# Gate strips of a Conformer-convolution layer loaded back through GpSimd's queue into four buffers

## The chip, the cores and the metric

One core of a Trainium2 chip runs the whole program. The metric is device time in microseconds (us) of one execution; for the kernel before, the median of 3 runs is 1468.54 us (1467.7 to 1470.9).

## The reference, cut to what matters

Two residual layers over 1040 tokens (16 meta tokens and 1024 others) of width 1024: a Conformer convolution, then differential attention, then a final RMSNorm. The change lies in the first layer:

```python
proj = h @ w_in                                   # 1024 -> 3 * 2048
u, g, z = split(proj, 3)
v = depthwise_causal_conv31(u * sigmoid(g)) + dw_bias
v = silu(layer_norm(v, ln_gain, ln_bias))         # over the 2048 channels
h = h + (v * silu(z)) @ w_out                     # 2048 -> 1024
```

`silu(z)` is the gate. It is needed only once the norm over all channels is known, so the kernel parks it in DRAM and loads it back.

## The kernel before, in words

Channels stand on partitions. The 2048 convolution channels are 16 strips (i or k, 0 to 15) of 128; the 1040 tokens are split by parity, and each parity half again into two halves n = 0 and 1 (HT = 520, QT = 260 elements). Every fp32 operand of a matmul is split in a high part (ScalarE copy, `wh`, `hi`) and a remainder (`lo_part`, L157, `wl`, `lo`), and `passes` (L207) multiplies high*high, high*low and low*high.

The first layer goes through these steps.

- Convolution, strips 0 to 15 (L457 to L534): TensorE makes the two projections, `vr{i}` holds the gated strip (tag `vr`, VR = 2 buffers), ScalarE and GpSimd make products and sums for part of the taps into `pb{i}` (tag `pa`, 2 buffers, L496 and L511), VectorE does the other taps (L524) and joins all (L526 to L528).
- Gates: `z_gate` (L431) projects z, applies SiLU and writes the strip to DRAM (`sz_d`, L441, from ScalarE's queue). Strips 0 to 11 are done beside the convolution, 12 to 15 after it (L587). The last, 15, is run strip by strip of the input (`release`), so that the buffers of the layer's input come free one by one.
- Norm: `mean` (L584), `center(0)` (subtract L558, square L563, sum `sq_sum` L564), `token_scale(0)` (`var_ps` L547, L573 to L578).
- First half, `y_part(k, 0)` (L596): for each even k one load `szr` brings two strips of the gate back (L601); each strip is scaled (L612), goes through SiLU (L613) and is multiplied by the gate (L621, all 16 on VectorE as `YM` says). `operand(0, k)` splits it into the two parts `b` (L638 on ScalarE, L639 by `lo_part` on VectorE).
- Output projection, half 0: strips m = 0 and 1 side by side, then m = 2 to 7, each 16 k of 6 matmuls (`multiply`, L655), residual added in `add_residual` (L664; `xr` is loaded on SP's queue, L666). Its weights take two strips each; the one numbered 50 (m = 0, k = 8 to 15) puts its remainder `wl50` into a buffer of tag `vr` (L182, `STW`).
- Beside half 0's projection, the norm of the other half, `center(1)` and `token_scale(1)` (L718), and then `y_part(k, 1)` and `operand(1, k)`, three or four k behind each m (`OK`, L736). Here 14 of the 16 products L621 are on GpSimd, those of k = 3 and k = 7 on VectorE. Tiles `y`, `xr` and `hsq` share three buffers (tag `xs`).
- Output projection, half 1, then the attention layer.

All DMAs that the table below names come from three queues: SP (weights `wf` L173, `szr`, `xr`), ScalarE's (`sz_d`) and GpSimd's (only in the attention layer and at the end, L968, L969, L1198). A queue runs its instructions in order, DMA issues too. A planner fixes that order when the program is built (`schedule_with_timeline_sim=True`): it runs a model of the engines and takes, on each, the ready instruction of the highest priority, which is program order moved forward by `high_priority` and held back by `issue_after`. Buffers of a tag are handed out in that order.

Of the kernel before, what the change touches and what calls it, by code (L numbers as in the profile page):

```python
# [12 lines left out]
F32 = mybir.dt.float32  # L13
# [6 lines left out]
P = 128  # L20
# [22 lines left out]
VR = 2  # L43
# [52 lines left out]
def trunk(  # L96
# [16 lines left out]
    V, A, G, PE, SP = nc.vector, nc.scalar, nc.gpsimd, nc.tensor, nc.sync  # L113
# [25 lines left out]
    def small(name, w, bufs=4):  # L139
        return scratch[-1].tile([P, w], F32, tag="sm", name=name, bufs=bufs)  # L140
# [164 lines left out]
    with ExitStack() as st0:  # L305
        sb = st0.enter_context(tc.tile_pool(name="sb0", bufs=1))
# [6 lines left out]
        def buf(tag, name, dt=F32, bufs=2):  # L313
            return sb.tile([P, T], dt, tag=tag, name=name, bufs=bufs)
# [106 lines left out]
        QT = HT // 2  # L421

        def part(t, n):

            return t.rearrange("p (two s) -> p two s", two=2)[:, :, n * QT : n * QT + QT]
# [31 lines left out]
        for i in range(CT):  # L457
            vr = sb.tile([P, 2, PAD + HT], F32, tag="vr", name=f"vr{i}", bufs=VR)
# [6 lines left out]
            with tc.high_priority(offset=HP):  # L465
                for ci, ((c0, w, o), (_, _, u)) in enumerate(zip(gates, ups)):
                    s = small(f"sig{i}", w=w)
# [128 lines left out]
        def y_part(k, n, last):  # L596
            i = k
            if k % 2 == 0:
                szr.append(sb.tile([P, 2, 2, QT], F32, tag="pa", name=f"szr{k}_{n}", bufs=2))
                with tc.issue_after(*loads[-1:]) if loads else ExitStack():  # L600
                    load = SP.dma_start(  # L601
                        out=szr[-1].rearrange("p i two s -> p i (two s)"),
                        in_=sz_d[n, i : i + 2].rearrange("i p c -> p i c"),
                    )
                loads.append(load.ins)
            s = szr[-1][:, k % 2]
            t = part(v_t[i], n)
            src = t
            if n:
                t = sb.tile([P, 2, QT], F32, tag="xs", name=f"y{k}_{n}", bufs=3)  # L610
            with tc.issue_after(done[-LOOK]) if n else ExitStack():
                y_mult.append(V.tensor_tensor(out=t, in0=src, in1=part(ln_r, n), op=ALU.mult).ins)  # L612
            silu = A.activation(  # L613
                out=t, in_=t, func=AF.Silu, scale=chn[:, i, TAPS + 1 : TAPS + 2],
                bias=chn[:, i, TAPS + 2 : TAPS + 3],
            ).ins
            y_silu.append(silu)
            if last:
                with tc.issue_after(silu):
                    A.preload_act_table_set("natural_log_exp_and_others")  # L620
            (V if n * CT + k in YM else G).tensor_tensor(out=t, in0=t, in1=s, op=ALU.mult)  # L621
            return t

        szr, loads, y_silu, y_mult = [], [], [], []

        def operand(n, ks):

            for k in ks:
                full = y_part(k, 1, k == CT - 1) if n else full0[k]
                if n:  # L630
                    t = sb.tile([P, 2, HT], F32R, tag="big", name=f"b{n}_{k}", bufs=16)
                else:
                    if k % 2 == 0:
                        twos.append(hn(f"b{n}_{k}", (P, 2, 2, HT), last=k == CT - 2))
                    t = twos[-1][:, k % 2]
                b[n].append((t[:, 0], t[:, 1]))
                hi, lo = nat(t[:, 0]), nat(t[:, 1])
                A.activation(out=hi, in_=full, func=AF.Copy)  # L638
                done.append(lo_part(V, lo, full, hi.bitcast(F32)).ins)  # L639
# [63 lines left out]
        for k in range(CT + LEAD):  # L703
            if k < CT:
                full0.append(y_part(k, 0, False))
            if k >= LEAD:
                operand(0, [k - LEAD])
# [35 lines left out]
    with ExitStack() as st1:  # L743
        sb = st1.enter_context(tc.tile_pool(name="sb1", bufs=1))
# [554 lines left out]
```

## Time and profile before

| | |
|---|---|
| median of 3 runs | 1468.54 us |
| profiled execution | 1467.64 us |
| its span | 1465.5 us |
| TensorE busy, share of the span | 97% |
| VectorE, ScalarE, GpSimd busy | 76%, 61%, 55% |
| mean granted TensorE clock | 0.991 |
| the 16 `szr` loads, 520 KB each, SP's queue | issued from 504.2 to 678.0 us |

The profile is of one execution; its span is the time from the first to the last instruction, and 2.1 us lie around it. An idle time of an engine is named with what ended it. A busy TensorE is not TensorE at its peak, since its matmuls are pipelined.

### The profile page before, as it was taken

What the parts mean: (1) busy time and instruction counts of PE and PEld (TensorE: products, weight loads), DVE (VectorE), ACT (ScalarE), POOL (GpSimd) and SP (SyncE); (2) the same over time, 40 slices, a digit from 0 to 9 for tenths busy, and PEclk for the clock granted to TensorE, in tenths of its full rate; (3) what the DMA queues carried; (4) which work ended last, traced back from release to release, by engine and by line L of the source; (5) the groups of instructions that cost most, each with busy time, mean ns of one, the idle gap of its engine ahead of it and who ended that gap; (6) DMA issues with size and microseconds to landing.
All of it is one profiled execution on the core that took longest, in us unless ns stands there. A gap on an engine that the chain in (4) does not pass through costs nothing.

```text
span 1465.5 us, 24123 instructions
## 1 busy us (share of the span) xinstructions
PE 1423.4 (97%) x8828; PEld 1333.3 (91%) x8828; DVE 1115.3 (76%) x2100; ACT 887.3 (61%) x1615; POOL 811.7 (55%) x646
## 2 busy tenths in 40 slices
PE   8999999999999999999999999999999999999997
PEld 7999999999999999899999878988889899897786
DVE  7989899899899988979545311578788787786774
ACT  7565665565555658766324411568778777786652
POOL 4598999999999940035014500525345354353572
PEclk9999999999999999999999999999999999999998
DMA  5021112112211333554443634223221322338532
GB/s 182 30 73 44 58 52 66 44 44 67 64 44 44 102 108 95 190 166 147 165 167 124 204 99 125 59 73 106 84 81 62 114 80 77 109 88 296 166 121 95
DMA packets 79928, 150.82 MB, mean 103 GB/s; under 512 B 6977, under 2 KB 46402, under 8 KB 78786
## 3 DMA queue, kind: packets, MB, share of 16 engines
q1 hardware_dynamic: 66706, 126.69, 27.3%
q0 software_dynamic: 3824, 13.37, 2.8%
q10 hardware_dynamic: 9280, 9.23, 2.0%
q8 instruction: 69, 1.13, 0.3%
q14 instruction: 49, 0.40, 0.1%
HBM read 106.73 MB, written 34.01 MB: 96 GB/s over the span
## 4 chain that ended last, share of the span: by engine, by line
PE 47%; POOL 18%; DVE 14%; ACT 8%; issue 8%; DMA 4%; SPq 1%; POOLq 0%; DVEq 0%; ACTq 0%
POOL pb L511 16%; PE c L207 8%; PE v L207 6%; PE k L207 5%; PE q L207 4%; PE za L207 4%; PE ao L207 3%; PE o L207 3%; PE u L207 3%; PE z L207 2%; DVE wl L157 2%; PE s L989 2%; ACT pr L510 2%; PE s L990 2%; PE tp L1023 2%
## 5 line engine op out<-in xcount | busy, mean ns | idle before, releaser
L511 POOL TENSOR_TENSOR pb<-pr,pb 128x521 f32<-128x521 f32 (+1 forms) x272 | 389.2, 1440 | 24.9 <-ACT pr L510 10.4
L510 ACT ACTIVATE pr<-vr,chn 128x521 f32<-128x521 f32 x224 | 150.6, 725 | 122.5 <-POOL pb L511 122.1
L207 PE MATMUL c<-b,wh 128*128 128x260 f32 x1024 | 187.3, 285 | 3.0 <-DVE b L157 1.9
L524 DVE SCALAR_TENSOR_TENSOR ev<-vr,chn,ev 128x520 f32<-128x520 f32 x240 | 181.2, 755 | 1.2
L189 ACT ACTIVATE wh<-wf 128x1024 fp32r<-128x1024 f32 x115 | 121.0, 1053 | 99.6 <-PE c L207 54.0
L207 PEld LDWEIGHTS c<-b,wh 128*128 128x128 f32 x1024 | 159.7, 191 | 3.8 <-DVE b L157 2.1
L207 PE MATMUL g<-hp,wh 128*128 128x346 f32 (+1 forms) x752 | 151.8, 329 | 7.6 <-ACT hp L383 3.6
L207 PE MATMUL u<-hp,wh 128*128 128x346 f32 (+1 forms) x752 | 155.9, 321 | 2.0 <-ACT wh L189 2.0
L207 PE MATMUL c<-b,wl 128*128 128x260 f32 x512 | 145.4, 286 | 3.8 <-DVE wl L157 3.8
L157 DVE TENSOR_TENSOR wl<-wf,wh 128x1024 fp32r<-128x1024 f32 x81 | 118.4, 1463 | 30.3 <-ACT wh L189 29.5
L157 POOL TENSOR_TENSOR wl<-wf,wh 128x1024 fp32r<-128x1024 f32 x34 | 85.7, 2521 | 92.9 <-ACT wh L189 47.4
L207 PEld LDWEIGHTS g<-hp,wh 128*128 128x128 f32 x752 | 127.6, 193 | 9.5 <-ACT hp L383 3.9
L207 PE MATMUL z<-hp,wh 128*128 128x346 f32 (+1 forms) x768 | 135.6, 321 | 0.5 <-ACT sig L469 0.5
L524 DVE SCALAR_TENSOR_TENSOR od<-xs,wc,od 128x520 f32<-128x520 f32 x176 | 132.6, 754 | 0.0
L696 POOL TENSOR_TENSOR total<-hsq,total 128x520 f32<-128x520 f32 x12 | 20.6, 1714 | 196.2 <-ACT hsq L695 196.2
L207 PEld LDWEIGHTS u<-hp,wh 128*128 128x128 f32 x752 | 125.7, 188 | 2.8 <-ACT wh L189 2.8
L207 PEld LDWEIGHTS z<-hp,wh 128*128 128x128 f32 x768 | 124.3, 188 | 0.9 <-ACT sig L469 0.7
L997 ACT ACTIVATE p<-p,st 128x272 f32<-128x272 f32 (+7 forms) x128 | 100.5, 785 | 39.3 <-DVE st L992 38.8
L207 PEld LDWEIGHTS c<-b,wl 128*128 128x128 f32 x512 | 97.7, 191 | 4.6 <-DVE wl L157 4.4
L207 PE MATMUL g<-hp,wl 128*128 128x346 f32 (+1 forms) x376 | 84.2, 322 | 0.0
L207 PE MATMUL v<-wv,g 128*128 128x512 f32 x352 | 83.5, 394 | 0.0
L989 PE MATMUL s<-k,q 128*128 128x256 f32 (+6 forms) x224 | 77.2, 349 | 5.3 <-DVE st L992 5.3
(292 smaller groups left out, 3465.1 us busy)
## 6 DMA issues: line engine op xcount, KB each, us to landing
wf<-conv_in SPq DMA_DIRECT2D x48, 512.0 KB, 3.5
wf<-conv_out SPq DMA_DIRECT2D x32, 512.0 KB, 4.1
wf<-attn_in SPq DMA_DIRECT2D x32, 512.0 KB, 3.8
wf<-attn_out SPq DMA_DIRECT2D x17, 512.0 KB, 3.7
sz_d<-sz ACTq DMA_DIRECT2D x32, 260.0 KB, 4.4
szr<-sz_d SPq DMA_DIRECT2D x16, 520.0 KB, 4.4
v<-v_d POOLq DMA_DIRECT2D x8, 1024.0 KB, 5.3
ya_d<-yb SPq DMA_DIRECT2D x28, 256.0 KB, 2.5
```

The costliest lines, as they stand in the source:

```text
L157: return eng.tensor_tensor(out=out_, in0=full, in1=hi, op=ALU.subtract)
L189: A.activation(out=wh, in_=wf, func=AF.Copy)
L207: PE.matmul(o, a[k], b[k], start=start and i == 0, stop=stop and i == tot - 1)
L510: A.activation(out=d, in_=src, func=AF.Copy, scale=w)
L511: G.tensor_tensor(out=dst, in0=d, in1=dst, op=ALU.add)
L524: V.scalar_tensor_tensor(out=dst, in0=src, scalar=w, in1=dst, op0=ALU.mult, op1=ALU.add)
L696: (V if SQA[m] == "V" else G).tensor_tensor(out=total[:, ns], in0=sq, in1=total[:, ns], op=ALU.add)
L989: PE.matmul(o[:, :wm], q2[m][:, qs], k2[m][:, c0 : c0 + wm], start=True, stop=False)
L990: PE.matmul(o[:, :wm], q2[m][:, qs], kl2[m][:, c0 : c0 + wm], start=False, stop=True)
L997: A.activation(out=p[:, :n], in_=p[:, :n], func=AF.Exp, scale=-1.0, bias=least, accum_out=st[:, 1:2],)
L1023: PE.transpose(tp[:, (kb - kb0) * P : (kb - kb0 + 1) * P], p0[:, kb * P : (kb + 1) * P], ident)
```

## The change

In the first half (n = 0) the loads of k = 2, 6, 10 and 14 go into buffers of tag `vr`, those of k = 0, 4, 8 and 12 stay in tag `pa`, so that four buffers of two strips serve the eight loads. In the second half all eight stay in `pa`. All sixteen loads are issued on GpSimd's queue in place of SP's.

```diff
         def y_part(k, n, last):
             i = k
             if k % 2 == 0:
-                szr.append(sb.tile([P, 2, 2, QT], F32, tag="pa", name=f"szr{k}_{n}", bufs=2))
+
+                if n == 0 and k % 4:
+                    szr.append(buf("vr", f"szr{k}_{n}", bufs=VR).rearrange("p (i two s) -> p i two s", i=2, two=2))
+                else:
+                    szr.append(sb.tile([P, 2, 2, QT], F32, tag="pa", name=f"szr{k}_{n}", bufs=2))
                 with tc.issue_after(*loads[-1:]) if loads else ExitStack():
-                    load = SP.dma_start(
+                    load = G.dma_start(
                         out=szr[-1].rearrange("p i two s -> p i (two s)"),
                         in_=sz_d[n, i : i + 2].rearrange("i p c -> p i c"),
                     )
```

## Rows read from the trace of the kernel before

**Rows 1.** The page, busy time of TensorE over the whole span

```profile
PE 1423.4 (97%) x8828; PEld 1333.3 (91%) x8828; DVE 1115.3 (76%) x2100; ACT 887.3 (61%) x1615; POOL 811.7 (55%) x646
```

**Rows 2.** Stretches: length, busy us (count) of PE, PEld, DVE, ACT, POOL, clock, DMA

```profile
590.50:594.60 4.10, 1.07 (x5) 0.42 (x3) 4.10 (x8) 4.05 (x7) 0.00 (x0) 0.87 0.60 182
594.60:600.20 5.60, 5.58 (x26) 5.59 (x27) 5.60 (x8) 4.24 (x7) 0.00 (x0) 0.50 0.87 290
600.20:624.00 23.80, 23.80 (x200) 23.80 (x200) 22.82 (x35) 14.02 (x21) 0.00 (x0) 1.00 0.58 184
...
692.00:694.00 2.00, 0.97 (x8) 0.97 (x9) 2.00 (x2) 1.98 (x2) 1.17 (x1) 1.00 0.05 10
```

**Rows 3.** Timeline of TensorE: start, length, instruction, [idle before it, what ended it]

```profile
592.28 0.39 PE L207 MATMUL c<-b,wh 128*128 128x260 f32 x1 [0.90 <-ACT wh L189]
594.62 0.59 PE L207 MATMUL c<-b,wh 128*128 128x260 f32 x1 [1.94 <-DVE b L157]
...
693.03 0.39 PE L207 MATMUL c<-b,wl 128*128 128x260 f32 x1 [2.23 <-DVE wl L157]
```

**Rows 4.** Timeline of VectorE, 579.9 to 623.8 us

```profile
579.91 2.52 DVE L621 TENSOR_TENSOR v<-v,szr 128x520 f32<-128x520 f32 x4
582.36 4.96 DVE L558 TENSOR_TENSOR v<-v,mean 128x520 f32<-128x520 f32 x8
...
588.38 3.74 DVE L558 TENSOR_TENSOR v<-v,mean 128x520 f32<-128x520 f32 x6
592.04 1.91 DVE L621 TENSOR_TENSOR v<-v,szr 128x520 f32<-128x520 f32 x3
593.87 0.69 DVE L157 TENSOR_TENSOR b<-v,b 128x520 fp32r<-128x520 f32 x1
...
597.54 2.35 DVE L157 TENSOR_TENSOR wl<-wf,wh 128x1024 fp32r<-128x1024 f32 x2
...
604.08 1.29 DVE L621 TENSOR_TENSOR v<-v,szr 128x520 f32<-128x520 f32 x2
...
616.73 7.05 DVE L564 TENSOR_TENSOR sq_sum<-sq_sum,lsq 128x520 f32<-128x520 f32 x9
```

**Rows 5.** Timeline of ScalarE, the high parts of the first operands

```profile
585.72 1.24 ACT L638 ACTIVATE b<-v 128x520 fp32r<-128x520 f32 x2
```

**Rows 6.** Timeline of SP's queue, DMA issues

```profile
581.25 1.59 SPq L601 DMA_DIRECT2D szr<-sz_d  x2
...
651.44 0.38 SPq L601 DMA_DIRECT2D szr<-sz_d  x1
```

**Rows 7.** Timeline of GpSimd around the first half and in the second

```profile
508.50 20.43 POOL L511 TENSOR_TENSOR pb<-pr,pb 128x521 f32<-128x521 f32 x14
...
629.55 1.31 POOL L696 TENSOR_TENSOR total<-hsq,total 128x520 f32<-128x520 f32 x1 [99.23 <-ACT hsq L695]
...
671.72 5.28 POOL L621 TENSOR_TENSOR y<-y,szr 128x520 f32<-128x520 f32 x3
```

**Rows 8.** Line 1198, loads issued by GpSimd: count, ns min/median/max

```profile
L1198 POOL DMA_DIRECT2D a<-ya_d x7: 713/721/818, 1364.1 to 1382.2; - x7
...
DMA to landing us min/median/max: 4.4/5.8/7.0
```

**Rows 9.** The chain that ended last, 626 to 701 us: start, length, what

```profile
626.28 0.88 PE var_ps L547 x4
...
652.85 4.02 DMA xr<-xn
...
661.12 1.82 DVE y L612
...
665.77 2.75 DMA xr<-xn
...
669.90 0.69 DVE y L612
...
699.43 1.15 DVE wl L157
```

## The prediction

> **What bounds the kernel now.** I read the page first, then stretches of 20 us around the loads, then the timelines of the engines in the bad stretches, and last the chain of waits. TensorE is busy for 97% of the span [rows 1], so a change off TensorE counts only where TensorE waits. Near the changed loads there are two such places. The first is the start of the output projection: from 590.50 to 594.60 us TensorE does 1.07 us of work, and in the next 5.60 us it does 26 matmuls at a clock of 0.50, half of full speed [rows 2]. What ends the longest idle time there is the first remainder `b` on VectorE [rows 3]. The second is the start of half 1, around 693 us, where TensorE waits 2.23 us for weights that VectorE prepares late [rows 3], and the clock stays at 1.00 [rows 2].
>
> Why is the first remainder late? On VectorE stand four gate products, fourteen subtractions of the *other* half (L558, in two lots with one weight remainder between), three more gate products, and only then, at 593.87, the first remainder [rows 4]. Its high part had been made by ScalarE at 585.72 [rows 5]. The products of k = 4 to 6 could not stand earlier: the `szr` for k = 4 was issued at 581.25, once the products of k = 0 and 1 had freed one of the two buffers [rows 6], so the planner filled VectorE with other work.
>
> **The change part by part.** *Four buffers in the first half.* The first four loads need the buffers of the last two `pb` and the last two `vr`, which come free with the end of the convolution; GpSimd's sums for it end at 508.50 + 20.43 = 528.9 us [rows 7]. Strips 0 to 7 are then in place long before the first product at 579.91, and products 4 to 7 can follow 0 to 3 directly. That does not by itself move the first remainder: the subtractions dropped behind the products may simply fill the rest of the gap, since the remainder also needs its high part in the planner's own account. What surely can leave is the three products directly ahead of it, 593.87 - 592.04 = 1.83 us [rows 4]. Bounds: nothing, if the planner puts subtractions in that place; the whole gap, 4.10 us less about 0.36 us for the three matmuls done in it [rows 2, 3], if the remainder follows its high part. I take 1.83 us, the piece that the released loads account for.
>
> *The clock.* With 1.83 us less, the longest wait of 1.94 us is nearly gone and 0.90 us is left [rows 3]; an idle time of 2.23 us kept the clock at 1.00 [rows 2, 3]. So I expect no fall. At full clock a matmul takes 23.80 / 200 = 0.119 us; 26 of them take 3.1 us in place of 5.60, which saves 2.5 us [rows 2]. Together TensorE would be 4.3 us ahead.
>
> *What is late next.* VectorE is busy for 22.82 of 23.80 us up to 624 us [rows 2], and the change takes no work off it. It ends the squares' sum of half 1 at 616.73 + 7.05 = 623.78 [rows 4], and TensorE reads that sum in `var_ps` at 626.28 [rows 9]. A TensorE that comes 4.3 us sooner waits there for the sum: 626.28 - 623.78 = 2.5 us can be kept, 1.8 are given back. From there to 699.43 the chain hardly touches TensorE; it runs through products, remainders, the `xr` loads and the additions [rows 9], so what arrives there early stays early and nothing more comes. Gain of the first half: 2.5 us.
>
> *GpSimd's queue, first half.* A load of this kind keeps GpSimd for 0.72 us (713 to 818 ns) [rows 8]; its rows in DRAM are about as long. Eight are 5.8 us inside an idle time of 99.23 us [rows 7]: nothing, as long as none goes ahead of the last convolution sums. If two did (strip 14's buffers are free before that), GpSimd's last sums, 20.43 us without a gap [rows 7], would end 1.4 us later, and the norm with them. The load of strips 14 and 15 waits on GpSimd for the last gate to reach DRAM; behind it stand only loads of the second half and the sum at 629.55. Landing takes 5.8 us [rows 8]; the four strips that are already there cover it.
>
> *GpSimd's queue, second half.* The first two loads again fall in the idle time; six stand between products and sums: 6 x 0.72 = 4.3 us on GpSimd at most. Where GpSimd is idle next, they cost nothing; the three products at 671.72 run without a gap [rows 7], and the load that needs the second of them freed would stand before the third: 0.7 us on the chain. Bounds 0 and 4.3; I take 0.7.
>
> *SP's queue.* Sixteen issues leave it. The weights behind them I cost at nothing: their loads wait for buffers that VectorE's weight remainders release, and VectorE is no earlier. An `xr` load may gain: at 652.85, behind the `szr` of 651.44 [rows 6], it took 4.02 us, at 665.77, with more distance, 2.75 [rows 9]. Two loads stand so close, 2 x 1.27 = 2.5 us at most, and nothing if the bytes of `szr` delay them from the other queue as well. I take 0.7 us, nearer to nothing, since the bytes still move in the same microseconds.
>
> *Sum.* -2.5 + 0.7 - 0.7 = -2.5 us. The profiled execution took 1467.64 us, span 1465.5 and 2.1 around it; that is 0.9 below the median of 1468.54. Against it the forecast is 1465.1, in terms of the median **1466.0 us**. About 0.2% (2.9 us) is what a measurement of this kernel can tell from no change, so the forecast lies just inside.
>
> **The rivals.** *The lead is kept whole.* If the remainder follows its high part and the planner also finds the other half's sum earlier, the whole 4.10 - 0.36 + 2.5 = 6.2 us stay: 1462.3. For it: VectorE has eight microseconds between high part and remainder [rows 4, 5]. Against it: VectorE has hardly any idle time up to 624 us [rows 2].
>
> *Nothing moves.* The fourteen subtractions stay ahead of the remainder, only shuffled with the products; then the change does not do what it says: 1468.5, give or take a shift of 3 us when the planner orders later work anew.
>
> *The wait moves to `wl50`.* (slower) Tag `vr` also has to house `wl50`, written as the second of the two remainders from 597.54 [rows 4]. If loads 10 and 14 hold both buffers, it must wait for product 11, which ends at 604.08 + 1.29 = 605.4 [rows 4]; with its 1.2 us it is there at 606.6. TensorE reaches k = 8 of m = 0 after 78 matmuls; 26 are done at 600.20, so today it is there at 606.4, and 4.3 us ahead at 602.1. The idle time of 4.5 us is over the 4.10-us stretch in which the clock fell [rows 2], so the half clock comes back: 0.2 + 2.5, and 0.7 for GpSimd, makes +3.4: 1471.9. It decides as soon as product 11 ends later than about 601 us. For it: two buffers, three claimants. Against it: products 8 to 11 can come sooner too, and load 14 cannot start before the last gate is written.
>
> *GpSimd becomes the wait.* (slower) VectorE's scaling at L612 takes 0.69 us alone and 1.82 beside a GpSimd product [rows 9]; the two shut each other out. If the issue of a load is shut out likewise, it costs 0.72 + 1.13 = 1.85 us; six are 11.1 us, and if half of them lie on the chain that is 5.5, against the gain of 2.5: +3.0, 1471.5. Against it: the seven loads of L1198 spread only from 713 to 818 ns [rows 8] with VectorE at work beside them. The Trainium skill, SBUF — State Buffer, section "SBUF: two separate sides", warns of this: while VectorE runs an operation in a two-port mode, GpSimd cannot write the descriptors of its loads, and it advises the hardware queues instead. By its example, some 620 ns alone and 3100 beside such an operation, six loads would be longer by 15 us (an estimate from that page). The rows of L1198 speak against that here, but they lie in another stage.
>
> **How the numbers follow.** The forecast has 0.36, half of it beyond 0.2% (its own range is -1 to -4.5 us: 1464.0 to 1467.5). The whole lead has 0.20, all faster. Nothing moves has 0.18: 0.12 same, 0.03 each side. `wl50` has 0.18: 0.14 slower, 0.04 same. GpSimd has 0.08, slower. So faster 0.18 + 0.20 + 0.03 = 0.41, same 0.34, slower 0.25. The range goes from just under the whole lead (1461.5) to just over the `wl50` case (1472.0); the far sides of those two and most of the GpSimd case are what is left out.
>
> **What would show it.** Right: four `szr` issues on GpSimd right after 529 us, eight gate products in one lot at about 580, the first remainder before 592.5, a clock of 1.00 from 594 to 600, `var_ps` at about 624 with TensorE waiting before it. Wrong: the first remainder still near 594 with the clock at 0.50 (nothing moves); an idle time ended by `wl` near 602 to 606; issues on GpSimd far over 0.8 us, or ahead of the last sums; TensorE's wait at 693 us grown by more than 2 us, which would mean that the chain of half 1 did not come sooner.

## The result, and the profile after

The changed kernel takes 1477.16 us (median of 6 runs, 1474.78 to 1479.14) against 1467.57 us for the kernel before (6 runs, 1465.95 to 1470.9): a ratio of 1.0064, 95% interval 1.0054 to 1.0075, so 8 to 11 us slower. The forecast was 1466.0 us, in a range of 1461.5 to 1472.0: wrong in sign, and outside the range.

The profiled execution took 1476.67 us, its span is 1474.7. Lines of the changed functions stand four further down (L621 is now L625, L601 is L605, L638 is L642); `center` and the helpers above it keep theirs. The page has the same TensorE share as [rows 1]:

```profile
PE 1427.2 (97%) x8828; PEld 1334.6 (90%) x8828; DVE 1120.3 (76%) x2100; ACT 886.8 (60%) x1615; POOL 821.9 (56%) x662
```

GpSimd has 16 instructions more and 10 us more of work. The time is lost elsewhere, as the positions below show. The stretches of [rows 2], in the same columns:

```profile
590.50:594.60 4.10, 0.33 (x3) 0.07 (x1) 4.10 (x8) 4.10 (x9) 0.00 (x0) 0.96 0.80 273
594.60:600.20 5.60, 3.22 (x13) 2.92 (x14) 5.60 (x11) 5.58 (x10) 0.00 (x0) 0.50 0.03 7
600.20:624.00 23.80, 23.80 (x196) 23.67 (x195) 22.50 (x33) 13.42 (x20) 2.16 (x3) 0.98 0.51 178
```

The gap at the start of the projection has grown: from 594.60 to 600.20 only 13 matmuls are done where there were 26, and the half clock (0.50) is still there. TensorE's timeline, as in [rows 3], says what ends the idle time now:

```profile
590.54 0.28 PE L207 MATMUL c<-b,wh 128*128 128x260 f32 x1
595.94 0.58 PE L207 MATMUL c<-b,wh 128*128 128x260 f32 x1 [5.11 <-ACT sz L437]
597.57 0.80 PE L207 MATMUL c<-b,wh 128*128 128x260 f32 x2 [1.04 <-ACT wh L189]
```

It is no longer the first remainder but ScalarE's copies `sz` of the last gate strip out of PSUM, where the matmuls leave their results. VectorE, to be read beside [rows 4]:

```profile
581.86 1.92 DVE L625 TENSOR_TENSOR v<-v,szr 128x520 f32<-128x520 f32 x3
...
585.52 2.53 DVE L625 TENSOR_TENSOR v<-v,szr 128x520 f32<-128x520 f32 x4
...
589.71 4.98 DVE L558 TENSOR_TENSOR v<-v,mean 128x520 f32<-128x520 f32 x8
...
595.81 0.71 DVE L157 TENSOR_TENSOR b<-v,b 128x520 fp32r<-128x520 f32 x1
...
604.88 1.93 DVE L558 TENSOR_TENSOR v<-v,mean 128x520 f32<-128x520 f32 x3
...
617.00 6.26 DVE L564 TENSOR_TENSOR sq_sum<-sq_sum,lsq 128x520 f32<-128x520 f32 x8
623.84 1.23 DVE L157 TENSOR_TENSOR wl<-wf,wh 128x1024 fp32r<-128x1024 f32 x1 [0.58 <-ACT wh L189]
624.98 3.11 DVE L564 TENSOR_TENSOR sq_sum<-sq_sum,lsq 128x520 f32<-128x520 f32 x4
```

Eight products stand early, as the early loads allow. But most of the subtractions of half 1 have moved behind them, three even to 604.88, and the sum of its squares now ends at 624.98 + 3.11 = 628.1 in place of 623.8. A weight remainder stands ahead of the last four additions. ScalarE shows why; the first two lines are from the kernel before, whose last square lies ahead of that weight's high part `wh`:

```profile
621.40 0.64 ACT L563 ACTIVATE lsq<-v 128x520 f32<-128x520 f32 x1 [0.16 <-DVE sq_sum L564]
623.20 1.06 ACT L189 ACTIVATE wh<-wf 128x1024 fp32r<-128x1024 f32 x1 [1.16 <-PE c L207]
```

and the same place after:

```profile
593.22 2.33 ACT L642 ACTIVATE b<-v 128x520 fp32r<-128x520 f32 x4
595.44 1.13 ACT L437 ACTIVATE sz<-z 128x348 f32<-128x348 f32 x3
...
620.88 0.64 ACT L563 ACTIVATE lsq<-v 128x520 f32<-128x520 f32 x1 [0.16 <-DVE sq_sum L564]
622.74 1.06 ACT L189 ACTIVATE wh<-wf 128x1024 fp32r<-128x1024 f32 x1 [1.23 <-PE c L207]
623.71 1.68 ACT L563 ACTIVATE lsq<-v 128x520 f32<-128x520 f32 x3
625.71 0.64 ACT L563 ACTIVATE lsq<-v 128x520 f32<-128x520 f32 x1 [0.32 <-DVE sq_sum L564]
```

The `wh` waits until TensorE lets go of a weight buffer, and four squares, which need nothing of TensorE, wait behind it.

The sum is read by `var_ps` (L547) on TensorE, and there too the order has changed. The first line is from the kernel before, the second from the changed one:

```profile
626.12 1.04 PE L547 MATMUL var_ps<-sq_sum,ones 128*128 128x260 f32 x4
631.41 1.04 PE L547 MATMUL var_ps<-sq_sum,ones 128*128 128x260 f32 x4
```

Neither names an idle time: TensorE does not wait for the sum, which has ended 2.3 and 3.3 us earlier; `var_ps` starts when its place in TensorE's order is reached. Ahead of it stand 244 matmuls of the output projection before and 269 in the changed kernel.

GpSimd's timeline (compare [rows 7]) has a second cause, the first two issues inside the convolution:

```profile
505.03 1.68 POOL L605 DMA_DIRECT2D szr<-sz_d  x2
...
510.36 20.64 POOL L511 TENSOR_TENSOR pb<-pr,pb 128x521 f32<-128x521 f32 x14
531.08 2.17 POOL L515 TENSOR_TENSOR pb<-pb 128x520 f32<-128x520 f32 x1
```

In the second half there is a third. The chain of waits (compare [rows 9]) now runs through a slower `xr` load, 5.02 us, and slower remainders `b`:

```profile
646.50 5.02 DMA xr<-xn
...
658.93 4.00 DMA xr<-xn
...
670.41 2.36 DVE b L157
...
682.97 2.33 DVE b L157
```

How these add up is seen from four events, read from VectorE's timeline of each kernel: the start of `ln_x` (L577) for half 0, the end of the squares' sum of half 1 (L564), the start of `ln_x` for half 1, and the start of the output projection's last addition (L671 before, L675 after). The third column is the ratio less 1, times the median of the kernel before in the same comparison.

| kernel | ratio to before | us | ln_x 0 | sum 1 ends | ln_x 1 | last addition |
|---|---|---|---|---|---|---|
| before | | | 567.54 | 623.78 | 630.61 | 787.36 |
| the change | 1.0064 [1.0054, 1.0075] | +9.4 | 570.62 | 628.09 | 635.70 | 795.49 |
| e1 buffers only | 1.0034 [1.0023, 1.0045] | +5.0 | | | | |
| e11 the same | 1.0058 [1.0044, 1.0073] | +8.5 | 568.63 | 629.40 | 637.03 | 795.11 |
| e15 the same | 1.0038 [1.0024, 1.0052] | +5.6 | 567.31 | 626.17 | 633.77 | 793.36 |
| e2 queue only | 1.0028 [1.0015, 1.0041] | +4.1 | 569.92 | 625.04 | 630.59 | 793.37 |
| e3 first load held | 1.0050 [1.0032, 1.0068] | +7.3 | 568.03 | 627.97 | 635.34 | 795.83 |
| e4 second half on SP | 1.0044 [1.0030, 1.0058] | +6.5 | 570.83 | 628.57 | 636.15 | 794.01 |
| e5 fill in the convolution | 1.0026 [1.0016, 1.0035] | +3.8 | 571.25 | 626.38 | 632.13 | 788.48 |
| e6 second half on GpSimd | 1.0016 [1.0006, 1.0025] | +2.3 | 567.84 | 624.09 | 630.80 | 791.25 |
| e7 buffers, early squares | 1.0017 [1.0007, 1.0026] | +2.5 | 568.03 | 626.49 | 633.31 | 790.82 |
| e8 early remainder | 1.0050 [1.0033, 1.0067] | +7.3 | 567.65 | 627.20 | 633.94 | 792.10 |
| e9 early squares, held, SP | 1.0019 [1.0009, 1.0029] | +2.8 | 568.08 | 626.09 | 632.95 | 789.68 |
| e10 before, early squares | 1.0018 [1.0008, 1.0027] | +2.6 | 568.12 | 624.83 | 632.09 | 789.54 |
| e12 buffers, `wh` behind | 1.0015 [1.0002, 1.0028] | +2.2 | 568.22 | 624.93 | 632.25 | 790.18 |
| e13 the change, `wh` behind | 1.0039 [1.0024, 1.0054] | +5.7 | 570.61 | 626.33 | 632.92 | 792.08 |
| e14 e13, held, SP | 1.0004 [0.9994, 1.0013] | +0.6 | 567.33 | 624.41 | 630.14 | 788.90 |

Where the convolution is left as it was, `ln_x 0` lies between 567.3 and 568.6: one profile is good to about a microsecond of position. The positions are of one execution each (that of e15, 1476.86 us, was the longest of its five), so ratio and last addition differ, by up to 2.7 us (e5).

`ln_x 1` follows the start of `var_ps` by 3.7 to 4.5 us in every trace, and no trace names an idle time of TensorE directly ahead of `var_ps`. It stands behind 244 matmuls of the projection in the kernel before, e2, e5, e6 and e12 to e14 (626.03 to 628.81), behind 268 or 269 in the change, e3, e4, e11 and e15 (629.39 to 632.62), and behind 247, 247, 239 and 260 in e7, e9, e10 and e8 (629.58, 629.21, 627.80, 630.20).

### The profile page after: what moved, and what is told of

It is laid out like the page before. It is cut to its first block, busy times and chain, and to the rows that moved or that the text cites. A ratio compares the mean times of both kernels' runs of the same rounds, so it can differ in the third digit from the quotient of the medians.

```text
span 1474.7 us, 24143 instructions
## 1 busy us (share of the span) xinstructions
PE 1427.2 (97%) x8828; PEld 1334.6 (90%) x8828; DVE 1120.3 (76%) x2100; ACT 886.8 (60%) x1615; POOL 821.9 (56%) x662
## 4 chain that ended last, share of the span: by engine, by line
PE 50%; POOL 17%; DVE 12%; issue 8%; ACT 8%; DMA 4%; SPq 0%; POOLq 0%; DVEq 0%; ACTq 0%
POOL pb L511 16%; PE c L207 8%; PE v L207 6%; PE k L207 6%; PE q L207 6%; PE za L207 5%; PE o L207 3%; PE ao L207 3%; PE u L207 3%; ACT pr L510 2%; PE z L207 2%; PE s L993 2%; PE s L994 2%; PE tp L1027 2%; DVE wl L157 2%
```

## The experiments

**The two parts of the change alone.** e1, and again e11 and e15: the four buffers, with every load on SP.

```diff
-                    load = G.dma_start(
+                    load = SP.dma_start(
```

> Four buffers in the first half, all loads on SP's queue as before. Three readings of the +9.6 us. Convolution: all of it comes from the two loads that GpSimd issues inside the convolution, whose end is 2.9 us later; then this kernel takes the time of before, 1467.6 (within 3 us). Buffers: the four buffers make the planner order VectorE's work of the two halves anew, and that order costs 4 us or more; then 1472 to 1477. Second half: GpSimd's loads between its products cost 3 us or more; then the time of before. My own guess is a sum of all three, about 3 + 4 + 2.6, so 1471 to 1472 here.

> The four buffers alone again, for a trace of it. Theory (early loads let the planner put products ahead of half 1's subtractions and squares): convolution and ln_x of half 0 as before (567.5, within 0.3 us), no load inside the convolution that delays it, the squares' sum of half 1 ends at 627 to 628.5 in place of 623.8, ln_x of half 1 near 634.5 to 635.5, and the projection's last addition 4 to 5 us later than before (787.4). Rival (the lost time comes from the loads themselves, which now land beside the convolution's traffic): ln_x of half 0 later by 2 us or more, and half 1 later by no more than that.

> The four buffers alone, beside the three others on the same chip, since the two earlier comparisons gave +5.0 and +9.3 us. If the parts add up (buffers 5, queue 4): ratio 1.003 to 1.004. If the buffers alone make nearly the whole loss: ratio 1.005 to 1.007. Its place for ln_x of half 1 should be 635 to 637 either way.

The profiled execution of e1 took 5547.5 us, so its trace is not used. The three comparisons give +5.0, +8.5 and +5.6 us; that of e11 is the outlier, and why is not settled. The traces of e11 and e15 show the same order of work. The convolution and half 0's norm are where they were, and half 1's sum ends late. ScalarE in e11:

```profile
619.75 0.64 ACT L563 ACTIVATE lsq<-v 128x520 f32<-128x520 f32 x1 [0.17 <-DVE sq_sum L564]
624.06 1.06 ACT L189 ACTIVATE wh<-wf 128x1024 fp32r<-128x1024 f32 x1 [3.66 <-PE c L207]
625.02 1.68 ACT L563 ACTIVATE lsq<-v 128x520 f32<-128x520 f32 x3
```

and in e15:

```profile
618.44 0.64 ACT L563 ACTIVATE lsq<-v 128x520 f32<-128x520 f32 x1 [0.17 <-DVE sq_sum L564]
620.83 1.06 ACT L189 ACTIVATE wh<-wf 128x1024 fp32r<-128x1024 f32 x1 [1.75 <-PE c L207]
621.79 1.68 ACT L563 ACTIVATE lsq<-v 128x520 f32<-128x520 f32 x3
```

The same `wh` stands in the middle of the squares; it waited 3.66 us for TensorE in the one and 1.75 in the other, so what it costs may swing with how late TensorE is.

e2: the queue alone, two buffers.

```diff
-                    load = SP.dma_start(
+                    load = G.dma_start(
```

> All loads on GpSimd's queue, two buffers as before. Convolution: the first load still goes ahead of the last convolution sums, so most of the loss stays: 1474 to 1477. Buffers: near the time of before, 1468 to 1471. Second half: at least 3 us slower than before, 1471 or more. As a sum of three: about 1473.

+4.1 us. One load (0.92 us at 505.04) stands in the convolution and `ln_x 0` is 2.4 us later, but `ln_x 1` is not: what this kernel loses at the last addition, 6.0 us, it loses in the second half. Buffers and queue together, 5.0 to 5.6 and 4.1, make about the 9.4 of the change; with the 8.5 of e11 they would make 12.6.

**The queue, place by place.** e3: the change, with the first load held behind the convolution's last sum.

```diff
+                conv_end = G.tensor_tensor(out=cp, in0=odd[:, 1:], in1=cp, op=ALU.subtract).ins
...
+                with tc.issue_after(loads[-1] if loads else conv_end):
```

> As changed, but the first load may not be issued before GpSimd's last sum of the convolution. Convolution: the end of the convolution is back at its time of before, and so is the total, 1468. Buffers, second half: 1474 or more, since only some 3 us come back. As a sum of three: about 1474, with the first remainder 3 us earlier than in the changed kernel.

`ln_x 0` is back at 568.03, yet +7.3 us and `ln_x 1` at 635.34 stay: the late convolution alone explains little of the change. e5 puts a delay of that kind into the kernel before, by twelve small writes to an unused tile on GpSimd ahead of the last sums:

```diff
+                if i == CT - 1 and not fill:
+                    for _ in range(FILL):
+                        with tc.issue_after(fill[-1] if fill else g_op):
+                            fill.append(G.memset(junk, 0.0).ins)
```

> The kernel before, with twelve small memsets on GpSimd ahead of its last convolution sums, where the changed kernel has its first two load issues; they should end the convolution some 1.5 to 3 us later, and nothing else is changed. If the later end of the convolution is what costs, the total grows by as much, to 1470 to 1472. If it is taken up before the second half's norm, as the run with the held loads suggests (there the convolution ended in time, and the output projection still ended 8.5 us late), the total stays within 1 us of before.

The norm of half 0 is 3.7 us later, of which 1.5 are left at `ln_x 1` and 1.1 at the last addition; the run is 3.8 us slower by the ratio. Profile and runs do not agree on how much of such a delay comes through: between a third and all of it. The fill itself took 2.36 us; 0.85 more comes from the last subtraction, which the delay moves beside a weight remainder on VectorE (2.15 us in place of 1.30; see the last section).

e4: the change with the second half's loads on SP. e6: the kernel before with only these on GpSimd. The edit of e4:

```diff
-                    load = G.dma_start(
+                    load = (SP if n else G).dma_start(
```

> As changed, but the loads of the second half go back to SP's queue. Convolution, buffers: no better than the changed kernel, 1476 to 1478. Second half: 3 us or more come back, 1471 to 1474. As a sum of three: about 1474.5.

> The kernel before, with only the loads of the second half moved to GpSimd's queue; VectorE's order around the halves is that of before. If GpSimd's load issues between products push the chain of products, remainders and additions, each issue that stands directly ahead of a product costs its 0.7 us and a bit more in the remainder that then meets the product: 2 to 4 us, 1470 to 1472. If they fall in idle time: the time of before.

e4 gives back 2.9 of the 9.4 us (1.5 at the last addition), and e6 costs 2.3, with 3.9 at the last addition and `ln_x 1` unmoved. In e6 VectorE's order is that of the kernel before, so its lines can be laid side by side. SP's queue, the chain of waits and VectorE's timeline of the kernel before:

```profile
639.43 0.38 SPq L601 DMA_DIRECT2D szr<-sz_d  x1
...
641.26 4.04 DMA xr<-xn
...
664.39 1.96 DVE L157 TENSOR_TENSOR b<-y,b 128x520 fp32r<-128x520 f32 x2 [0.86 <-ACT b L638]
...
676.01 1.55 DVE L157 TENSOR_TENSOR b<-y,b 128x520 fp32r<-128x520 f32 x1 [1.45 <-ACT b L638]
```

GpSimd's timeline of e6, a product and the load behind it, and a later product:

```profile
639.55 1.31 POOL L621 TENSOR_TENSOR y<-y,szr 128x520 f32<-128x520 f32 x1
640.80 0.74 POOL L601 DMA_DIRECT2D szr<-sz_d  x1
...
679.22 1.32 POOL L621 TENSOR_TENSOR y<-y,szr 128x520 f32<-128x520 f32 x1
```

The chain of waits of e6, the same `xr`:

```profile
641.46 5.92 DMA xr<-xn
```

And VectorE's timeline of e6, the remainders that GpSimd's products now fall on:

```profile
666.26 2.96 DVE L157 TENSOR_TENSOR b<-y,b 128x520 fp32r<-128x520 f32 x2 [0.84 <-ACT b L638]
...
678.81 2.31 DVE L157 TENSOR_TENSOR b<-y,b 128x520 fp32r<-128x520 f32 x1 [1.47 <-ACT b L638]
```

On SP the load of this strip was issued at 639.43, ahead of `xr`; on GpSimd it stands behind a product, comes at 640.80, and the `xr` issued 0.7 us later takes 1.9 us longer; that the bytes of the two loads get in each other's way is argued from these times, not tested. Further on, an issue of 0.74 us pushes a product onto VectorE's remainder: the pair at 666.26 takes 2.96 us where it took 1.96, the one at 678.81 takes 2.31 where it took 1.55. Together 1.9 + 1.0 + 0.8 = 3.7 us, nearly the 3.9 of the table.

**The order on VectorE.** e7: the four buffers, and half 1's subtractions and squares raised in priority. e10: the same in the kernel before. e9: e7 with the changed kernel's loads, the first held as in e3, the second half's on SP.

```diff
-        center(1, [added[0], y_mult[CT - 1]])
+        with tc.high_priority(offset=400):
+            center(1, [added[0], y_mult[CT - 1]])
```

> Four buffers, loads on SP's queue, and the subtractions and squares of the second half with a priority 400 higher, so that VectorE does fourteen of the subtractions ahead of the products. If the four buffers cost their 5 us because the squares' sum of the second half ends late, it ends here within 1 us of its time of before (623.8 us) and the total is 1467 to 1469.5. If the buffers cost by something else, the total stays at 1472 to 1475.

> The kernel before, with nothing but the priority of half 1's subtractions and squares raised by 400. Theory (half 1's norm sets the pace of what follows, and in the kernel before it already stands about as early as VectorE allows, its squares' sum ending at 623.8): at most 1 us either way at ln_x of half 1 (630.6 before), the time within 0.2% of the kernel before. Rival (any earlier squares are worth their time): ln_x of half 1 earlier by 2 to 4 us, near 627.5, and the time 2 to 4 us less, ratio near 0.998. Rival (the squares push the first half's remainders back and TensorE loses what they gain): ln_x at 632 or later, time up by 2 us or more.

> The changed kernel with three things put back at once: no load of the first half before the convolution's last sum, the loads of the second half on SP, and the squares of half 1 given back their early place on VectorE (priority raised by 400). Theory (three parts that add up, each with its own place): what stays is the half of the buffers' cost that the raised priority did not recover, some 2.5 us: ratio near 1.0017, 1469.5 to 1471, the squares' sum of half 1 ends near 626, ln_x of half 1 near 633.5. Rival (the parts act on each other, or a GpSimd load in the first half has a cost that neither hold nor place takes away): over 1473, ratio above 1.003.

All three land at +2.5 to +2.8 us. With the subtractions first, TensorE waits some 4.5 us for the first high part (4.45 at 595.70 in e10), and no `ln_x 1` comes before 632. So the subtractions' place can give back half of the buffers' cost, and in the kernel before, where nothing was lost, the same edit costs 2.6 us: the second rival of e10's text, not its theory.

e8: the kernel before, half 1's subtractions held so that the first remainder comes early. It asks whether the lead of TensorE, on which the forecast was built, is worth anything.

```diff
-        center(1, [added[0], y_mult[CT - 1]])
+        center(1, [added[0], done[0]])
```

> The kernel before, loads and buffers as they were, but the subtractions of the second half may not start before the first remainder is made. TensorE then starts the output projection about 4 us sooner and at full clock. If TensorE's lead is kept: 1462 to 1465. If the second half's chain on VectorE sets the pace, so that the squares' sum ends as late as in the changed kernel, the lead is given back and more: 1469 to 1474.

The first remainder starts at 586.91 in place of 593.87. TensorE still idles 1.33 and 2.43 us, and the program is 7.3 us slower: the sum of half 1 ends 3.4 us later and the last addition is 4.7 later. But the edit did not give TensorE a lead that lasts. Its 35 matmuls of the projection by 600.20 us, against 29 before, had become 122 against 128 by 612 us, after a wait of 0.71 us for a weight remainder at 602.23, and another of 1.23 followed at 614.26. So e8 shows that an earlier first remainder is not worth what it pushes back; what a lead that is kept would bring, no run shows.

**The one high part.** The edit of e12 to e14 names only the weights of m = 2 and later, whose high part goes behind the last square and whose remainder goes behind the last sum. In the kernel before, this edit leaves every engine's order as it is. In the changed one the planner then orders more than these weights anew (below). e12 is with the buffers alone, e13 in the whole change, e14 in the change with the first load held and the second half on SP.

```diff
-                    added[:] = [V.tensor_tensor(out=tot, in0=tot, in1=sq, op=ALU.add).ins]
+                    added[:] = [V.tensor_tensor(out=tot, in0=tot, in1=sq, op=ALU.add).ins, sq_op]
...
-            with tc.high_priority(offset=CP):
+            with tc.issue_after(added[0]), tc.issue_after(added[1]), tc.high_priority(offset=CP):
                 return [weights.get(), weights.get()]
```

> The four buffers alone, and the high part of the first weights of m = 2 put behind the last square of half 1 on ScalarE (with its remainder behind the last of the sums on VectorE). Theory (what the four buffers cost is this one place: a high part that waits for TensorE stands ahead of the last four squares): the sums go on without a break from about 616.6, eleven by 0.79, and end near 625.3; ln_x of half 1 near 632, 5 us sooner than with the buffers alone (637.0); time 1 to 3 us above the kernel before, ratio 1.0007 to 1.002. Rival (TensorE needs those weights as much as the norm needs the squares): ln_x comes sooner but TensorE waits 2 us or more for the remainder of m = 2 near 628, and the projection's end stays 6 us or more above the kernel before, ratio above 1.003.

> The whole change, with the same high part behind the last square. Theory: the part of the change that comes from this place, 4 to 5 us, goes: ln_x of half 1 near 631.5 to 632.5 in place of 635.7; the issues on GpSimd still cost their 2 to 4 us in the second half; time 3 to 5.5 us above the kernel before, ratio 1.002 to 1.0038. Rival (the late convolution and the late first remainder set half 1's norm, not the place of that high part): ln_x stays above 634.5 and the ratio above 1.0045.

> The change with all three causes taken out: the first load held behind the convolution's last sum, the second half's loads on SP, the high part behind the last square. Theory (these three are the whole of it): 0 to 2 us above the kernel before, ratio 1.000 to 1.0014, ln_x of half 1 630.5 to 632. Rival (something more, such as the half clock at the start of the projection, costs time of its own): ratio above 1.002 with ln_x above 632.5.

VectorE's timeline of e12: the last eleven sums run on without a break, and the weight's remainder follows.

```profile
616.19 8.74 DVE L564 TENSOR_TENSOR sq_sum<-sq_sum,lsq 128x520 f32<-128x520 f32 x11
624.85 1.22 DVE L157 TENSOR_TENSOR wl<-wf,wh 128x1024 fp32r<-128x1024 f32 x1
```

ScalarE's timeline of e12, the last square and the high part behind it:

```profile
622.55 0.64 ACT L563 ACTIVATE lsq<-v 128x520 f32<-128x520 f32 x1 [0.17 <-DVE sq_sum L564]
623.10 1.04 ACT L189 ACTIVATE wh<-wf 128x1024 fp32r<-128x1024 f32 x1
```

The buffers cost 2.2 us now in place of 5.6 on the same chip, and the change 5.7 in place of 9.4. The unbroken sum is only about half of that: counted from `ln_x 0`, it ends 2.2 us sooner than in e15, and 1.8 sooner in e13 than in the change. The rest came with it. From the last square to the end of the projection, VectorE, ScalarE and GpSimd run in e12 in the order of the kernel before, and `var_ps` stands behind 244 matmuls again. In e15 it stands behind 268, the norm's first step on ScalarE (L573) stands behind two squares that wait for residual additions, and weight remainders and products on VectorE are ordered otherwise. What each of these costs, the runs do not separate.

With all three causes out, e14 is within 0.1% of the kernel before (+0.6 us, interval -0.9 to +1.9). Its buffers and its first-half loads on GpSimd are those of the change, so nothing that stays in it costs, or brings, anything that can be measured. In e13 `ln_x 1` came at 632.92, a little later than the 632.5 expected, and the ratio 1.0039 is just over the 1.0038 named. No kernel of the study is faster than the one before.

## Why the prediction was wrong, step by step

**The released loads.** "What surely can leave is the three products directly ahead of it, 1.83 us." The loads did come early and the products did move up, as said. With the buffers alone the first remainder follows the mean (L584) after 592.42 - 534.26 = 58.16 us (e15), against 593.87 - 534.48 = 59.39 before: 1.2 us sooner, two thirds of the step. But the wait changed its name: TensorE now waits for `sz` (2.34 us at 592.92 in e15, 5.11 in the change), because ScalarE's copies of the last gate strip stand behind high parts, four of them in one lot at 593.22 in the change. I asked what is late next on VectorE and not on ScalarE.

**The clock.** It did not stay up: 0.50 in the same stretch, 5.11 us of idle time ahead of it. The step hung on the one before.

**The cap, the step that failed most.** The text took the end of half 1's sum, 623.78, as fixed and let TensorE wait for it. It wrote that VectorE was full (22.82 of 23.80 us) and that fillers stand ahead of the remainder. Both were right, and what follows from them is that eight products moved ahead must push half 1's subtractions and squares back: the sum ended 4.3 us later, at 628.09. The step also missed where the pushed work meets other queues. ScalarE's `wh`, tied to TensorE, came to stand in the midst of the squares, and on TensorE 25 more matmuls, 25 x 0.119 = 3.0 us, came to stand ahead of `var_ps`. So TensorE, which was to wait there for the sum, came late instead: `var_ps` started at 631.41, where the forecast had 623.8. The longer idle time at the projection's start, 6.15 us in all against 3.04, makes the rest of its 5.3 us and a little more. e12 and e13 show what this new order of half 1's norm costs: 3.4 to 3.7 us of the time (5.6 less 2.2, and 9.4 less 5.7; each of these four is known to about 2 us). That the planner chose it because the subtractions came late is argued, not shown.

In the forecast's terms, the gain of 2.5 us from the four buffers was a loss of 5.0, 5.6 or 8.5 (e1, e15, e11).

**GpSimd, first half.** The condition was named ("none goes ahead of the last convolution sums") and then taken as met, though the kernel before issued its first loads at 504.2 us. Two issues went in, 1.68 us, and the price of 1.4 was half of what it came to: the last subtraction, L515, takes 2.17 us in place of 1.30 (the last section has the row of before), and `ln_x 0` is 3.1 us later. In time that is 2.1 us by e3 (9.4 less 7.3, whose intervals overlap) and 3.8 by e5.

**GpSimd, second half.** Taken at 0.7 us in bounds of 0 to 4.3; e6 measured 2.3 by the runs (0.9 to 3.7), and 3.9 at the last addition. The mechanism of an issue ahead of a product was right. What was left out is that the delayed product then falls on a remainder.

**SP's queue.** Taken at 0.7 us gained. The first `xr` behind a moved load lost: 5.02 us at 646.50, and 5.92 in e6, against 4.04; the later ones kept their times (4.00 at 658.93, against 4.02). The clause "nothing if the bytes of `szr` delay them from the other queue as well" fits this, and its worse side was not in the bounds.

**The rivals.** *Nothing moves* was right that most subtractions (eleven of the fourteen) stay ahead of the first remainder and that the half clock stays, and wrong about everything behind it. The *wl50* wait did not come: from 597.57 to 653.56 TensorE's timeline names no idle time. (Its sum takes 26 matmuls as done by 600.20; with the three before 594.60 they are 29, which makes its wait 0.4 us longer.) *GpSimd becomes the wait* had one of the right engines, and the sign, but not by its mechanism: the issues of the second half took 0.74 to 0.75 us, not 1.85. The Trainium skill, SBUF — State Buffer, section "SBUF: two separate sides", says that GpSimd cannot write the descriptors of such a load while VectorE runs an operation in a two-port mode; no issue here is longer than 0.92 us, and no run shows whether an operation beside them was in that mode. The same section of the Trainium skill says that a VectorE operation with two SBUF inputs and a GpSimd operation that reads SBUF exclude each other, and that the one that starts first goes first. L515 at 2.17 us agrees with that: it ends 1.2 us behind a weight remainder that started first (last section). The remainder of 2.31 us agrees in its end, 0.58 us behind the product's; but it starts at 678.81, ahead of the product at 679.22, and so do those of 2.36 and 2.33 us in the changed kernel; why they did not go first stays open. *The lead is kept whole* did not come, as TensorE's start was later and not earlier; e8, which was meant to test it, got no lead that lasts. One sign that the text named for a late half 1 did not come although half 1 was late: TensorE's wait near 693 us has not grown, but lies 7.9 us later (2.36 us at 700.91, against 2.23).

## What to carry to other kernels

Where a planner orders full engines, a load that comes earlier does not only release its own consumer: ask which work that consumer pushes back, and whether one instruction with a tie to another engine can come to stand in the middle of it. Follow the pushed work on every engine that it passes through, not only on the one that is full, and count what stands ahead of its reader there (269 matmuls in place of 244 here). A load moved to a computing engine's queue costs its issue (0.72 us here), and also the new meetings that the issue shifts its neighbours into (1.0 and 0.8 us here, and 1.9 in a transfer that ran beside the moved one).

## What was not expected of the hardware

GpSimd's timeline of the kernel before has the last subtraction of the convolution by itself:

```profile
529.02 1.30 POOL L515 TENSOR_TENSOR pb<-pb 128x520 f32<-128x520 f32 x1
```

VectorE's timeline of the changed kernel has the weight remainder that runs beside it:

```profile
530.27 1.82 DVE L157 TENSOR_TENSOR wl<-wf,wh 128x1024 fp32r<-128x1024 f32 x1 [0.73 <-ACT wh L189]
```

This 128x520 subtraction took 1.30 us alone and 2.17 beside a weight remainder on VectorE, which took 1.82 in place of 1.22 in turn; a remainder on VectorE took 0.69 us alone and 2.31 where a product of 1.32 ran on GpSimd.

An idle time of 2.23 us at 693 us left TensorE's granted clock at 1.00 [rows 2, 3], but in the changed kernel idle times of 1.35 and 1.77 us, 8 us apart, were followed by 0.72, and by 0.50 from 663 to 665 us. Two others as far apart, 2.36 us at 700.91 and 1.57 at 708.75, left it at 1.00 up to 720 us, so the length of the idle times alone did not tell what the clock did. TensorE's timeline of the changed kernel, and stretches of it in the columns of [rows 2]:

```profile
653.56 0.39 PE L207 MATMUL c<-b,wl 128*128 128x260 f32 x1 [1.35 <-DVE wl L157]
...
661.39 0.39 PE L207 MATMUL c<-b,wl 128*128 128x260 f32 x1 [1.77 <-DVE wl L157]
```

```profile
653.60:661.40 7.80, 6.03 (x49) 5.83 (x49) 6.46 (x7) 5.43 (x8) 5.11 (x5) 1.00 0.42 128
661.40:664.00 2.60, 2.60 (x16) 2.60 (x17) 2.15 (x5) 0.61 (x2) 0.00 (x0) 0.72 1.00 341
664.00:668.00 4.00, 4.00 (x28) 4.00 (x27) 4.00 (x4) 2.02 (x3) 3.39 (x2) 0.76 0.33 128
```
